# Three seams of layer 0: when the condition's SiLU, the latents' row sums and the next normalization's blocks are issued

## The chip, the cores and the metric

The kernel runs on one core of a Trainium2 chip, as one launch. The metric is device time in microseconds (us), the median of three runs. On the core, TensorE (PE in the profile; PEld is its loading of stationary operands) multiplies into PSUM, VectorE (DVE), ScalarE (ACT) and GpSimd (POOL) work on tiles in SBUF and PSUM, and SyncE (SP), POOL and ACT issue DMAs. Every engine takes its own instructions in a fixed order and waits on semaphores for the others.

## The reference

Two layers of a hybrid backbone over 1024 latent tokens and 256 context tokens, width 1024. Cut to layer 0, which the change touches, and to the start of layer 1:

```python
sh1, sc1, g1, sh2, sc2, g2 = split(silu(c) @ ada_w[0] + ada_b[0], 6)      # latents; context: the same with c_ctx
u = rms_norm(h, norm1_g[0]) * (1 + sc1) + sh1
y = concat(fourier_mix(u @ w_in), hyena_mix(u @ w_in)) @ w_out              # both streams
h = h + g1 * y
v = rms_norm(h, norm2_g[0]) * (1 + sc2) + sh2
h = h + g2 * ((silu(v @ w_gate) * (v @ w_up)) @ w_down)                      # FFN, inner width 2816 = 22 blocks of 128
u1 = rms_norm(h, norm1_g[1]) * (1 + sc1_of_layer_1) + sh1_of_layer_1         # layer 1: attention, FFN, final norm
```

`rms_norm` divides a token's row by the root of the mean of its squares.

## The kernel before

Activations lie transposed: 8 blocks (`b`) of 128 channels on the partitions, tokens along the free axis, in pieces `pc`: 0 and 1 are the two halves of the latents (512 tokens each), 2 is the context (256). Every operand of a product is split into a high part (`hi`, a cast to fp32r on ACT, line L350) and the rest (`lo = x - hi`, a subtraction on DVE, L352; `split`), and a product is three products: hi by hi, hi by lo, lo by hi. `weights` loads a block of weights into a staging tile and splits it; the parts are called `wh` and `wl` in the profile. `lin` (its products are L346) runs 8 blocks by 3 products, so 24 products a piece.

The program is one straight line, written with generators: a main loop calls `next()` on side work at chosen places. From the order in which instructions are traced, their dependencies and an estimate of their durations, a scheduler then fixes the order of each engine's instructions; `follow(x)` makes what is traced under it come behind instruction `x` on the engine of `x`.

Four stages of layer 0 matter here.

- **Output projection** (`out_proj`, 647 to 766 us in the profile). `inverse_last` ends the Hyena branch: its last operands `y` come from DVE sums (L1469 to L1475) and a split, so a cast on ACT, each. Then `out_proj` multiplies group 0, which is the context and latent half 0 together (products L1765, then L346), and group 1, latent half 1. `evict` (L1739) adds a result to `h` on DVE, and `square` (L609 on ACT, L614 on DVE) sums squares over the blocks. Each `fetch` takes one step of `late_groups`, which makes the modulation vector `m = 4` of layer 0: `load_cond` loads c and c_ctx into four broadcast tiles and applies SiLU to them on ACT (L556); then each of 8 blocks takes four row-wise products with sum on DVE (L584), with weights that POOL loads.
- **Second normalization.** `rms_begin` sums the squares over channels with 4 narrow products against a column of ones (`pq<-c,tk`), takes root and reciprocal; `rms_end` spreads the result to a 128-row tile (`pq<-t,c`, copied by ACT at L642). For latent half 1 both are called in `after1`, at the end of group 1, ahead of the FFN. `wino_first` and `wino_second` then form the FFN's operands of halves 0 and 1.
- **Context FFN** (22 blocks `fb`, 770 to 893 us): gate and up weights of each block, 24 products of 256 columns each, SiLU (L2011) and product (L2012). From `fb = 2` on, each block takes one step of `second`, the generator that runs `wino_second` (L1835, L1842, L1823 on DVE, a cast L1822 on ACT).
- **Context down projection** (1527 to 1595 us, products L2230): 22 blocks of 24 products, each with a weight block to split. `hook(kb)` takes one step of `after2(1)` in blocks 3, 6 and 8 on: the row sums, their spreading, and then the normalization of layer 1 for half 1, two of its 8 blocks in a step (`norm_block`: L656 on DVE, L658 on ACT, L659 on DVE).

Weight parts for the context FFN take tiles from the pools `wh`/`wl` (two each) and `ws` (four) in turn (`pair3`, counter `p3`).

Of the kernel before, what the change touches and what calls it, by code (L numbers as in the profile page):

```python
# [13 lines left out]
AF = mybir.ActivationFunctionType  # L14
# [244 lines left out]
class Builder:  # L259
# [333 lines left out]

    def late_groups(self, ms, where):

        self.load_cond(wide=where == "s4")
        for m in ms:
            yield from self.ada_group(0, m, (0, 1), where)

# [815 lines left out]
    def inverse_last(self, y, fl):  # L1415

        nc, a = self.nc, self.a
        V = nc.vector
        C, x, late = [], [], []

        def product(acc, first, cb, m, e, i, f):
            yh, yl = (q[:, cb * P:cb * P + P] for q in self.y_of(1, i, f))
            d = acc[cb][:, e * 256:e * 256 + 256]
            for k, (s, w) in enumerate(((yh, m[:, :256]), (yh, m[:, 256:]), (yl, m[:, :256]))):
                nc.tensor.matmul(d, s, w, start=cb not in first, stop=e == 1 and i == 1 and f == 3 and k == 2,  # L1425
                                 skip_group_check=True)
                first.add(cb)

        next(fl)
        for r in (0, 1):  # L1430
            acc = [self.PS() for _ in range(4)]
            first = set()
            ms = self.cmat2(a["vke_l"][r], True)
            for e, m in enumerate(ms):
                for cb in range(4):
                    for f in (0, 1):
                        product(acc, first, cb, m[:, f * 512:f * 512 + 512], e, 2 * e, 2 * r + f)
            yield
            if r == 0:
                next(fl)  # L1440
            else:
                for _ in fl:
                    yield
            ms = [self.cmat2(a["vko_l"][r, :, c:c + 2048], True) for c in (0, 2048)]
            if r:
                for cb in range(4):
                    x.append(self.S4())
                    self.ld(x[cb], self.xd[1][cb][:, :LAT])
            sa = [self.TK(), self.TK()]
            sa = [t[:, i:i + 256] for t in sa for i in (0, 256)]  # L1450
            for cb in range(4):
                for e, i in ((0, 3), (1, 1)):
                    for h, m in enumerate(ms[e]):
                        for f in (0, 1):
                            product(acc, first, cb, m[:, f * 512:f * 512 + 512], e, i, 2 * h + f)
                    if e == 0:
                        nc.scalar.copy(sa[cb], acc[cb][:, :256])
                A, B = sa[cb], acc[cb][:, 256:]
                t = self.G() if r == 0 else self.T()
                V.tensor_tensor(t[:, :256], A, B, ADD)  # L1460
                rv = t[:, 256:][:, ::-1]
                if r == 0:
                    V.tensor_tensor(rv, A, B, SUB)
                    C.append(t)
                    continue
                V.tensor_tensor(rv, B, A, SUB)
                y.t.update(self.new_act(pcs=(0, 1), wide=False, blocks=(4 + cb,)).t)
                v = self.T()
                V.tensor_tensor(v, C[cb], t, ADD)  # L1469
                V.tensor_tensor(C[cb], C[cb], t, SUB)  # L1470
                V.tensor_tensor(v, v, x[cb][:, :512], MUL)
                self.split(v, y.ap(0, 4 + cb, 0), y.ap(1, 4 + cb, 0))
            yield
        for cb in range(4):
            V.tensor_tensor(C[cb], C[cb], x[cb][:, 512:], MUL)  # L1475
            self.split(C[cb], y.ap(0, 4 + cb, 1), y.ap(1, 4 + cb, 1))

    def inverse_c(self, o, y):
        nc, a = self.nc, self.a
# [494 lines left out]
        s.to(2)  # L1974
        return s

    def ffn(self, l, u, h, hs, second, after, keep=None, begun={}):

        nc, a = self.nc, self.a
        n2 = NFB // 2  # L1980
# [19 lines left out]
        if l == 0:  # L2000
            self.pad(self.pt, PAD_T)
        if u is not None:
            for fb in range(NFB):
                wide = 3 if fb < NFB - 2 else 2
                gh, gl = self.weights(a["gate"][l, fb], wide=wide)
                uh, ul = self.weights(a["up"][l, fb], wide=wide)
                lo = self.last_lo
                ga = self.lin(gh, gl, 0, range(KB), u, (2,))[2]
                ua = self.lin(uh, ul, 0, range(KB), u, (2,))[2]
                t = self.T()  # L2010
                nc.scalar.activation(t[:, :256], ga[:, :256], AF.Silu)  # L2011
                nc.vector.tensor_tensor(t[:, :256], ua[:, :256], t[:, :256], MUL)  # L2012
                self.ldr(hidc[fb // 2][:, fb % 2], t[:, :256])
                if fb >= 2:
                    with self.follow(last):
                        next(second, None)
                last = lo
            self.load_cond(act=False)
            todo = (x for l1, m in [(0, 5)] + [(1, m) for m in range(6)]
                    for x in self.ada_group(l1, m, (0, 1) if l1 == 0 or m < 2 else (0,), "s4"))  # L2020
# [16 lines left out]
        for i in range(NFB // 2):  # L2037
# [26 lines left out]
            gate = dict(self.res)  # L2064
            for k in ((0, 0), (1, 1), (0, 1)):
                nc.scalar.activation(gate[k], gate[k], AF.Silu)
            t = self.G()
# [463 lines left out]
    def run(self):  # L2531
        nc, a = self.nc, self.a
# [9 lines left out]
        def drain(g):  # L2542
            for _ in g:
                pass

        u = Act()
# [90 lines left out]
        h = Act()  # L2637
        u = None

        def load_h(pcs):  # L2640
            for pc in pcs:
                for b, t in enumerate(self.load_x(pc)):
                    h.put(0, b, pc, t)

        uf = Act()
        hs0 = [self.DR([P, 1280]) for _ in range(KB)]
        hs1 = [self.DR([P, 1280]) for _ in range(KB)]

        def spill(h, hs, pcs):
            for pc in pcs:  # L2650
                for b in range(KB):
                    self.ldr(hs[b][:, pc * 512:pc * 512 + WID[pc]], h.ap(0, b, pc))

        rest = []

        def after1(pcs):
            spill(h, hs0, pcs)
            if 2 in pcs:
                uf.t.update(self.new_act(pcs=(2,)).t)
                rs = self.rms(pcs)  # L2660
                for b in range(KB):
                    self.norm_block({b: h.ap(0, b, 2)}, b, 2, 0, 3, uf, rs[0])
                load_h((1,))
                rest.append(rs[1])
            else:
                drain(first)
                rest.append(self.rms((1,))[0])

        def first_row():
            yield from self.wino_first(h, 0, 3, rest.pop())  # L2670

        first = first_row()

        load_h((2, 0))
        self.out_proj("w_out", y, [(2, 0), (1,)], h, 0, 2, after1, first, late)
        for b in range(8):
            self.tap(f"h1_{b}", h.ap(0, b, 0))
        u1 = Act()
        hd = [self.DR([P, LAT]) for _ in range(KB)]

        def after2(pc):
            c = self.rms_begin(pc)
            yield
            r = self.rms_end(pc, c)
            yield
            for b in range(KB):
                if b % 2 == 0:
                    u1.t.update(self.new_act(pcs=(pc,), blocks=(b, b + 1)).t)
                self.norm_block({b: h3.ap(0, b, pc)}, b, pc, 1, 0, u1, r)
                if b % 2:  # L2690
                    yield

        h3 = Act()
        self.ffn(0, uf, h3, hs0, (x for r in rest for x in self.wino_second(h, 0, 3, r)), after2, hd)
        for b in range(8):
            self.tap(f"h2_{b}", h.ap(0, b, 0))
        for i, _ in enumerate(self.values(u1)):
# [62 lines left out]
        for i, _ in enumerate(first_part(1)):  # L2760
            if i == 7:
                c = self.rms_begin(0)
# [53 lines left out]
        begun = {(0, 0): self.wino_begin(1, 0, 0, self.G)}  # L2816
        c = self.rms_begin(1)
# [87 lines left out]
```

## Time and profile before

| | |
|---|---|
| time, median of 3 runs (lowest, highest) | 2862.4 us (2861.56, 2863.65) |
| the profiled execution: time, span | 2867.56 us, 2865.8 us |
| granted TensorE clock, mean | 0.984 |
| busy: PE, PEld, DVE, ACT, POOL | 97%, 81%, 71%, 46%, 19% |
| 640.00 to 686.60 us: PE busy, clock | 43.61 of 46.60 us, 0.96 |
| 768.00 to 780.00 us: PE busy, clock | 11.39 of 12.00 us, 0.72 |
| 780.00 to 897.00 us: PE busy, clock | 117.00 of 117.00 us, 1.00 |
| 1545.00 to 1556.00 us: PE busy, clock | 8.00 of 11.00 us, 0.90 |

Times in the profile count from the first instruction. The clock is the share of its full speed that TensorE was granted in a stretch; at 0.50 a product takes twice as long. Columns of a stretch are, in order: from and to, length, then busy time and instructions of PE, PEld, DVE, ACT and POOL, the clock, the DMA share and GB/s.

### The profile page before, as it was taken

The numbers are of one execution on the slowest core, as the hardware profiler recorded it, in microseconds if no ns is written. First come the engines' busy times: TensorE is split into PE (matmuls) and PEld (weight loads), VectorE is DVE, ScalarE is ACT, GpSimd is POOL, SyncE is SP. The second block draws the span as 40 slices with busy tenths as digits, with TensorE's granted clock in tenths as the row PEclk, the third lists the DMA queues.
The fourth block names the chain that finished last, engine by engine and source line by source line (L and its number), as shares of the span: only waits on it lengthen the run. The fifth ranks groups of instructions, "written<-read, shape, count | busy, mean of one in ns | idle before, by whom it ended". The sixth has DMA issues, their size and how long they took to land.

```text
span 2865.8 us, 43630 instructions
## 1 busy us (share of the span) xinstructions
PE 2779.7 (97%) x15610; PEld 2325.6 (81%) x15610; DVE 2045.2 (71%) x3531; ACT 1321.0 (46%) x2269; POOL 543.2 (19%) x880
## 2 busy tenths in 40 slices
PE   7999999999999999999999999999999999999998
PEld 4876678788899888888888888888887788888887
DVE  6766777768777888866777536878867987655556
ACT  5433335443554333333455326888755533333434
POOL 2210234241001211222110002332212122112000
PEclk9999899999999999999999999999999999999999
DMA  7356525655556656658884436777856366434763
GB/s 267 120 167 214 158 83 190 220 172 219 204 189 210 207 192 200 212 196 328 308 308 154 147 120 143 195 203 200 227 199 215 122 242 224 144 110 167 234 195 133
DMA packets 296887, 554.21 MB, mean 193 GB/s; under 512 B 81872, under 2 KB 128658, under 8 KB 296670
## 3 DMA queue, kind: packets, MB, share of 16 engines
q1 hardware_dynamic: 232318, 361.06, 40.0%
q0 software_dynamic: 61504, 185.65, 18.6%
q10 hardware_dynamic: 2848, 4.72, 0.4%
q8 instruction: 123, 2.02, 0.3%
q14 instruction: 94, 0.77, 0.1%
HBM read 405.01 MB, written 118.76 MB: 183 GB/s over the span
## 4 chain that ended last, share of the span: by engine, by line
PE 71%; issue 3%; DVE 3%; DMA 2%; ACT 1%; POOL 1%; DVEq 0%; SPq 0%; POOLq 0%; ACTq 0%
PE ps L1932 25%; PE ps L346 15%; PE ps L2109 11%; PE pq L346 9%; PE pq L1932 3%; PE pq L2109 3%; PE ps L2230 2%; PE ps L2463 1%; PE ps L1425 1%; DMA s<-d 1%; DMA s<-in_c_ctx 1%; DMA g<-in_bias 0%; DMA s<-in_x_t 0%; DVE wl L352 0%; DVE s L352 0%
## 5 line engine op out<-in xcount | busy, mean ns | idle before, releaser
L1932 PE MATMUL ps<-s,s 128*128 128x512 f32 x2012 | 498.6, 391 | 3.3 <-DVE s L1823 1.7
L1932 PEld LDWEIGHTS ps<-s,s 128*128 128x128 f32 x2012 | 379.4, 189 | 83.9 <-DVE s L1823 2.6
L346 PE MATMUL ps<-s,wh 128*128 128x256 f32 (+1 forms) x1776 | 403.3, 331 | 6.0 <-ACT wh L350 2.5
L346 PEld LDWEIGHTS ps<-s,wh 128*128 128x128 f32 x1776 | 296.3, 191 | 41.3 <-ACT wh L350 3.4
L346 PE MATMUL ps<-s,wl 128*128 128x256 f32 (+1 forms) x888 | 267.1, 329 | 0.1
L2109 PE MATMUL ps<-s,s 128*128 128x512 f32 (+1 forms) x1000 | 259.7, 383 | 3.2 <-DVE s L352 3.1
L350 ACT CAST s<-s 128x1024 fp32r<-128x1024 f32 (+2 forms) x192 | 173.0, 926 | 192.0 <-DMA s<-d 172.3
L346 PE MATMUL pq<-s,wh 128*128 128x512 f32 (+1 forms) x848 | 260.9, 389 | 0.3 <-ACT wh L350 0.3
L352 DVE TENSOR_TENSOR wl<-ws,wh 128x1024 fp32r<-128x1024 f32 (+1 forms) x141 | 168.2, 1194 | 118.4 <-ACT wh L350 113.9
L350 ACT CAST wh<-ws 128x1024 fp32r<-128x1024 f32 (+1 forms) x141 | 144.7, 1026 | 204.4 <-PE ps L346 85.4
L346 PE MATMUL ps<-s,s 128*128 128x65 f16 (+4 forms) x2748 | 230.3, 235 | 6.3 <-DVE st L2446 2.6
L352 DVE TENSOR_TENSOR s<-s,s 128x1024 fp32r<-128x1024 f32 (+2 forms) x170 | 191.0, 1154 | 58.3 <-ACT s L350 58.2
L352 DVE TENSOR_TENSOR s<-t,s 128x512 fp32r<-128x512 f32 (+2 forms) x238 | 151.5, 652 | 104.6 <-ACT s L350 81.7
L350 ACT CAST s<-t 128x512 fp32r<-128x512 f32 (+2 forms) x238 | 133.8, 582 | 188.4 <-PE ps L1932 68.0
L2109 PEld LDWEIGHTS ps<-s,s 128*128 128x128 f32 x1000 | 184.4, 188 | 41.2 <-DVE s L352 4.8
L1932 PE MATMUL ps<-s,wh 128*128 128x512 f32 x624 | 194.8, 390 | 0.0
L346 PEld LDWEIGHTS ps<-s,wl 128*128 128x128 f32 x888 | 165.6, 190 | 16.6 <-DVE wl L352 0.6
L337 POOL DMA_DIRECT2D d<-s x186 | 101.4, 546 | 376.5 <-DVE s L1739 92.9
L346 PEld LDWEIGHTS pq<-s,wh 128*128 128x128 f32 x848 | 150.5, 189 | 22.8 <-issue 1.2
L346 PE MATMUL pq<-s,wl 128*128 128x512 f32 (+1 forms) x424 | 161.8, 382 | 1.3 <-DVE wl L352 1.3
L2109 PE MATMUL ps<-s 128*128 128x512 f32 (+1 forms) x500 | 150.7, 385 | 0.0
L346 PEld LDWEIGHTS ps<-s,s 128*128 128x128 f32 (+1 forms) x828 | 129.3, 192 | 22.3 <-issue 4.4
(487 smaller groups left out, 5485.8 us busy)
## 6 DMA issues: line engine op xcount, KB each, us to landing
s<-d SPq DMA_DIRECT2D x282, 256.0 KB, 3.9
d<-s POOLq DMA_DIRECT2D x170, 256.0 KB, 3.7
s<-in_down SPq DMA_DIRECT2D x150, 256.0 KB, 4.1
s<-in_ada_w POOLq DMA_DIRECT2D x64, 512.0 KB, 5.0
ws<-in_up SPq DMA_DIRECT2D x44, 512.0 KB, 3.7
d<-g POOLq DMA_DIRECT2D x86, 256.0 KB, 3.1
ws<-in_gate SPq DMA_DIRECT2D x42, 512.0 KB, 4.3
d<-tk POOLq DMA_DIRECT2D x66, 256.0 KB, 4.0
```

Source lines behind the costliest of these rows:

```text
L337: self.last_ldr = self.nc.gpsimd.dma_start(out, in_).ins
L346: self.last_mm = self.nc.tensor.matmul(o, l, r, start=st, stop=sp).ins
L350: self.last_hi = nc.scalar.copy(hi, src).ins
L352: self.last_lo = eng.tensor_tensor(lo, src, hi.bitcast(F32), SUB).ins
L1425: nc.tensor.matmul(d, s, w, start=cb not in first, stop=e == 1 and i == 1 and f == 3 and k == 2, skip_group_check=True)
L1932: nc.tensor.matmul(ps, x[:, sl], y, start=first and j == 0 and x is wh and y is xh, stop=j == 3 and x is wl, skip_group_check=True)
L2109: m = nc.tensor.matmul(acc[j][:, c0:c1], x[:, sl], y[:, xs], start=first and k == 0, stop=last and k == 2, skip_group_check=True)
L2230: m = nc.tensor.matmul(o, x[:, nb * P:(nb + 1) * P], t[:, c:c + 256], start=kb == 0 and k == 0 and nb % 2 == 0, stop=kb == NFB - 1 and k = ...
L2463: nc.tensor.transpose(ps[:, j * P:(j + 1) * P], src[:, j * P:(j + 1) * P], self.ident)
```

## The change

Three places of layer 0, all by the order in which work is traced; no product is added or removed.

1. `load_cond` in `late_groups` no longer applies SiLU. The SiLU comes three `fetch` steps later, and behind `inv_hi`, the last cast of `inverse_last`.
2. `rms_begin` and `rms_end` of latent half 1 move from `after1` into a new generator `second`, whose first two steps they are; each comes behind the last product traced so far (`last_mm`). `ffn` now takes a step of `second` from `fb = 0` on. The gate weights of `fb = 0` are loaded and split in step 6 of `wino_first` (`early`), still in `out_proj`; `p3 = 1` ahead of them gives them a pair of `ws` tiles.
3. In `after2(1)` a step normalizes one block, not two, and each block comes behind the `lo` of the block before on DVE.

```diff
     def late_groups(self, ms, where):
-        self.load_cond(wide=where == "s4")
+        self.load_cond(wide=where == "s4", act=False)
+        yield
+        yield
+        yield
+        with self.follow(self.inv_hi):
+            for t in self.cond:
+                for x in t:
+                    self.nc.scalar.activation(x, x, AF.Silu)
         for m in ms:
             yield from self.ada_group(0, m, (0, 1), where)
...
             self.split(C[cb], y.ap(0, 4 + cb, 1), y.ap(1, 4 + cb, 1))
+        self.inv_hi = self.last_hi
...
-    def ffn(self, l, u, h, hs, second, after, keep=None, begun={}):
+    def ffn(self, l, u, h, hs, second, after, keep=None, begun={}, early=()):
...
         if u is not None:
+            last = None
             for fb in range(NFB):
                 wide = 3 if fb < NFB - 2 else 2
-                gh, gl = self.weights(a["gate"][l, fb], wide=wide)
+                gh, gl = early.pop() if fb == 0 else self.weights(a["gate"][l, fb], wide=wide)
                 uh, ul = self.weights(a["up"][l, fb], wide=wide)
...
-                if fb >= 2:
-                    with self.follow(last):
-                        next(second, None)
+                with self.follow(last):
+                    next(second, None)
                 last = lo
...
-        rest = []
+        rest, early = [], []
...
                 drain(first)
-                rest.append(self.rms((1,))[0])
...
         def first_row():
-            yield from self.wino_first(h, 0, 3, rest.pop())
+            for k, _ in enumerate(self.wino_first(h, 0, 3, rest.pop())):
+                if k == 6:
+                    self.p3 = 1
+                    early.append(self.weights(a["gate"][0, 0], wide=3))
+                yield
...
             r = self.rms_end(pc, c)
             yield
+            los = []
             for b in range(KB):
                 if b % 2 == 0:
                     u1.t.update(self.new_act(pcs=(pc,), blocks=(b, b + 1)).t)
-                self.norm_block({b: h3.ap(0, b, pc)}, b, pc, 1, 0, u1, r)
-                if b % 2:
+                with self.follow(los.pop() if los and pc == 1 else None):
+                    self.norm_block({b: h3.ap(0, b, pc)}, b, pc, 1, 0, u1, r)
+                los.append(self.last_lo)
+                if b % 2 or pc == 1:
                     yield
 
         h3 = Act()
-        self.ffn(0, uf, h3, hs0, (x for r in rest for x in self.wino_second(h, 0, 3, r)), after2, hd)
+
+        def second():
+            with self.follow(self.last_mm):
+                c = self.rms_begin(1)
+            yield
+            with self.follow(self.last_mm):
+                r = self.rms_end(1, c)
+            yield
+            yield from self.wino_second(h, 0, 3, r)
+
+        self.ffn(0, uf, h3, hs0, second(), after2, hd, early=early)
```

The program keeps 15450 rows of PE, 3507 of DVE and 870 of POOL; ACT has 2187 rows where it had 2185, two more loads of an activation table, both in the context FFN. Away from the three places the engines' orders differ by a few rows only, at the very end of the program among them: there the 4 narrow products of the first of the last two row sums now stand 16 PE rows earlier.

Line numbers move: L609, L642, L656, L658, L659, L1739, L1822 before are L616, L649, L663, L665, L666, L1747, L1830 now.

On ACT at the end of the inverse (`s<-t` and `s<-g` are casts of `y`, `wh<-ws` casts of weights, rows with L556 or L603 the condition's SiLU), before:

```order
L350 CAST s_1523_6140<-t_6144 128x512
L556 ACT_TABLE_LOAD
L556 ACTIVATE s_1572_6234<-s_1572_6234 128x512 x2
L556 ACTIVATE s_1573_6239<-s_1573_6239 128x512 x2
L350 CAST s_1529_6178<-t_6182 128x512
L350 CAST s_1513_6066<-g_5480 128x512
L350 CAST wh_6356<-ws_6355 128x1024
```

and now:

```order
L350 CAST s_1523_6140<-t_6144 128x512
L350 CAST s_1529_6178<-t_6182 128x512
L350 CAST s_1513_6066<-g_5480 128x512
L350 CAST wh_6326<-ws_6325 128x1024
L350 CAST s_1519_6104<-g_5508 128x512
L350 CAST s_1525_6142<-g_5536 128x512
L350 CAST s_1531_6180<-g_5564 128x512
L603 ACT_TABLE_LOAD
L603 ACTIVATE s_1572_6234<-s_1572_6234 128x512 x2
L603 ACTIVATE s_1573_6237<-s_1573_6237 128x512 x2
```

The four SiLUs moved behind six casts, `s_1529`, which ends the operands of group 0, among them.

On PE, where the output projection meets the context FFN (`wh_7146` is its last weight, `pq` of width 1 the row sums, `ps` of 256 columns the gate products), before:

```order
L346 MATMUL ps_7219<-s_1531_6180,wl_7147 128x512
L346 MATMUL pq_7261<-c_91,tk_6978 128x1 x4
L346 MATMUL ps_7431<-s_1674_6862,wh_7420 128x256
L346 MATMUL ps_7431<-s_1675_6863,wh_7420 128x256
L346 MATMUL ps_7431<-s_1674_6862,wl_7421 128x256
```

and now, at the row sums' new place, 48 rows later (`ps_7440` are the up products of `fb = 0`, `ps_7489` the gate products of `fb = 1`):

```order
L346 MATMUL ps_7440<-s_1681_6869,wh_7410 128x256
L346 MATMUL ps_7440<-s_1680_6868,wl_7411 128x256
L346 MATMUL pq_7469<-c_91,tk_6978 128x1 x4
L346 MATMUL ps_7489<-s_1674_6862,wh_7478 128x256
L346 MATMUL ps_7489<-s_1675_6863,wh_7478 128x256
```

The row sums moved behind the 48 gate and up products of `fb = 0`. On ACT a little later, at the weights of `fb = 3` (`wh_7625`, its gate), before:

```order
L642 COPY t_7269<-pq_7274 128x512
L350 CAST wh_7558<-s_2061_7557 128x1024
L1822 CAST s_2069_7621<-s_1711_6980 128x512
L2011 ACTIVATE t_7547<-ps_7497 128x256
L350 CAST wh_7625<-s_2070_7624 128x1024
L1822 CAST s_2079_7692<-s_1725_7060 128x512
```

and now:

```order
L649 COPY t_7543<-pq_7548 128x512
L2020 ACTIVATE t_7613<-ps_7563 128x256
L1830 CAST s_2069_7621<-s_1711_6980 128x512
L1830 CAST s_2079_7692<-s_1725_7060 128x512
L350 CAST wh_7625<-s_2070_7624 128x1024
L350 CAST wh_7631<-s_2073_7630 128x1024
```

The gate weights of `fb = 3` now stand behind two casts of `wino_second`, and these behind the copy of the row sums.

On DVE in the context down projection (`wl` is a weight's low part, L656 or L663 the first step of a normalized block, L659 or L666 its last), before:

```order
L656 SCALAR_TENSOR_TENSOR t_14583<-s_3020_12687,c_99,t_14505 128x512
L656 SCALAR_TENSOR_TENSOR t_14587<-s_3021_12689,c_99,t_14505 128x512
L656 SCALAR_TENSOR_TENSOR t_14630<-s_3022_12691,c_99,t_14505 128x512
L656 SCALAR_TENSOR_TENSOR t_14634<-s_3023_12693,c_99,t_14505 128x512
L656 SCALAR_TENSOR_TENSOR t_14674<-s_3078_12968,c_99,t_14505 128x512
L659 SCALAR_TENSOR_TENSOR s_3328_14581<-t_14583,c_99,s_3328_14581 128x512
L352 TENSOR_TENSOR wl_14553<-ws_14551,wh_14552 128x1024
```

and now:

```order
L663 SCALAR_TENSOR_TENSOR t_14583<-s_3020_12687,c_99,t_14505 128x512
L666 SCALAR_TENSOR_TENSOR s_3328_14581<-t_14583,c_99,s_3328_14581 128x512
L352 TENSOR_TENSOR wl_14553<-ws_14551,wh_14552 128x1024
L663 SCALAR_TENSOR_TENSOR t_14624<-s_3021_12689,c_99,t_14505 128x512
L352 TENSOR_TENSOR wl_14596<-ws_14594,wh_14595 128x1024
L663 SCALAR_TENSOR_TENSOR t_14664<-s_3022_12691,c_99,t_14505 128x512
L666 SCALAR_TENSOR_TENSOR s_3329_14582<-t_14624,c_99,s_3329_14582 128x512
```

The weights' low parts moved ahead: two steps of the normalization stand before the first of them, six before.

## The prediction

> **What bounds the kernel now.** The page's first section comes first.
>
> ```profile
> PE 2779.7 (97%) x15610; PEld 2325.6 (81%) x15610; DVE 2045.2 (71%) x3531; ACT 1321.0 (46%) x2269; POOL 543.2 (19%) x880
> ```
>
> PE is the bound and the change keeps its products, so it can win only PE's idle time and the slow clock behind it. Then PE's waits, asked for each seam: between 636 and 686.5 us, 686.5 and 777.6, and 1300 and 1600 us (us in total, times, longest).
>
> ```profile
> PE ps L1765 <- ACT s L350: 2.3, 1, 2.3
> PE ps L1765 <- DVE wl L352: 0.3, 1, 0.3
> PE ps L1765 <- DVE s L1739: 0.3, 1, 0.3
> ...
> PE pq L346 <- DVE tk L614: 2.3, 1, 2.3
> ...
> PE ps L2230 <- DVE wl L352: 3.0, 2, 2.1
> ```
>
> Each seam has its own wait: a cast of `y`, the last sum of squares, a weight's low part. Then the view by stretches, which I laid on the steps of the clock; two late stretches without a seam stand at the end.
>
> ```profile
> 666.36:669.77 3.41, 1.32 (x8) 0.91 (x6) 0.00 (x0) 2.26 (x4) 0.00 (x0) 1.00 0.98 401
> 669.77:673.19 3.42, 3.23 (x9) 2.65 (x10) 3.25 (x9) 3.17 (x6) 0.00 (x0) 0.50 0.09 32
> 765.35:768.76 3.41, 1.12 (x7) 0.62 (x5) 1.44 (x2) 1.56 (x3) 0.54 (x1) 1.00 0.43 172
> 768.76:772.17 3.41, 3.41 (x17) 3.41 (x18) 2.99 (x4) 2.72 (x7) 0.00 (x0) 0.50 0.45 119
> 772.17:775.59 3.42, 3.42 (x18) 3.42 (x18) 1.99 (x3) 1.57 (x5) 0.00 (x0) 0.50 0.71 236
> 1547.00:1550.41 3.41, 2.50 (x22) 2.31 (x22) 3.41 (x5) 2.28 (x4) 0.00 (x0) 1.00 0.38 127
> 1550.41:1553.83 3.42, 1.32 (x13) 1.12 (x11) 3.42 (x6) 2.49 (x3) 0.00 (x0) 1.00 0.33 126
> 1553.83:1557.24 3.41, 3.41 (x16) 3.41 (x17) 3.41 (x5) 0.72 (x1) 0.00 (x0) 0.50 0.65 201
> 2072.65:2076.07 3.42, 1.92 (x10) 1.43 (x10) 2.77 (x6) 2.83 (x8) 2.89 (x6) 1.00 1.05 284
> 2157.99:2161.40 3.41, 2.08 (x10) 1.50 (x9) 3.41 (x7) 2.93 (x5) 2.14 (x5) 1.00 1.02 373
> ```
>
> A stretch of 3.41 us with PE busy 1.92 us or less is followed by one or two at clock 0.50; with 2.08 or 2.50 it is not (2157.99; 1547.00). So about 1.4 us of idle time within one stretch costs half of the next, 1.7 us, besides. The Trainium skill (TensorE: Matmul & The Clock Gate, section on why this matters) asks only that there be no idle gap over about 3 us. By that rule the gaps here would cost no clock; the rows show 0.50 behind gaps of 2.1 to 2.3 us, so the rows decide, and the rule is left as a rival below.
>
> **First seam: the SiLU, now behind the casts.** ACT, then DVE and PE:
>
> ```profile
> 657.99 1.28 ACT L556 ACT_TABLE_LOAD   x1
> 664.80 0.63 ACT L556 ACTIVATE s<-s 128x512 f32<-128x512 f32 x1 [5.53 <-DMA s<-in_c]
> 668.13 1.27 ACT L556 ACTIVATE s<-s 128x512 f32<-128x512 f32 x2 [0.78 <-DMA s<-in_c_ctx]
> 669.31 0.60 ACT L350 CAST s<-t 128x512 fp32r<-128x512 f32 x1
> ...
> 661.38 0.68 DVE L1471 TENSOR_TENSOR t<-t,s 128x512 f32<-128x512 f32 x1
> 683.21 0.75 DVE L584 CUSTOM_DVE_ANT_0 t<-s,s,c 128x512 f32<-128x512 f32 x1
> ...
> 683.88 1.53 DVE L1739 SCALAR_TENSOR_TENSOR s<-ps,c,s 128x256 f32<-128x256 f32 x3
> 691.14 1.22 DVE L352 TENSOR_TENSOR wl<-ws,wh 128x1024 fp32r<-128x1024 f32 x1
> ...
> 669.96 1.01 PE L1765 MATMUL ps<-s,wh 128*128 128x512 f32 x2 [2.28 <-ACT s L350]
> ```
>
> The last operand's sum is done at 662.1, but its cast stands behind SiLUs that wait for DMAs until 668.1. The Trainium skill agrees that ACT cannot pass a waiting instruction ("ACT/DVE are strict FIFO", same page, part 1). In the new order the cast runs at 662.1, and PE needs it at 667.7: the 2.28, the clock's 1.7 and the 0.3 behind it go, 4.3 in all.
>
> What is late next: the casts end about 666.8, table and SiLUs (1.28 + 4 x 0.59, since two took from 668.13 to 669.31) about 670.4, against 669.4 before, and the 32 products with sum (0.67 each in a row, 683.21 to 683.88) start then, three fetches later in the program, with evictions and weight parts between them. Counting DVE's new order from 670.4 (24 of the 32, 8 evictions of 0.5 (1.53 for three), 4 sums and one weight part, no idle time), the low part of the weights of `nb = 5` ends at 691.5; PE, without its stall, has reached them at about 690. Ahead of that, PE's order puts 4 products of `nb = 6` before the rest of `nb = 5`, whose weight tile is free only when `nb = 4` ends: about 0.6 and 0.45 us of idle time. Price from 0, if DVE is 2 us sooner, to 4.5, if SiLU is 2 us later and the clock falls too; I take 1.05, by the count. Loads by SP and POOL keep their order. Net -3.3.
>
> **Second seam: the row sums, now behind `fb = 0`.**
>
> ```profile
> 768.61 1.76 PE L346 MATMUL pq<-c,tk 128*128 128x1 f32 x8 [2.29 <-DVE tk L614]
> 770.22 0.77 PE L346 MATMUL ps<-s,wh 128*128 128x256 f32 x2
> 776.58 1.02 PE L346 MATMUL pq<-t,c 128*128 128x512 f32 x2
> ...
> 767.20 0.63 ACT L609 ACTIVATE tk<-s 128x512 f32<-128x512 f32 x1 [2.96 <-DVE s L1739]
> 767.74 1.97 ACT L350 CAST wh<-s 128x1024 fp32r<-128x1024 f32 x2
> 778.20 0.58 ACT L642 COPY t<-pq 128x512 f32<-128x512 f32 x1
> 780.33 0.62 ACT L1822 CAST s<-s 128x512 fp32r<-128x512 f32 x1
> ...
> 768.79 2.36 DVE L352 TENSOR_TENSOR wl<-s,wh 128x1024 fp32r<-128x1024 f32 x2 [0.24 <-ACT wh L350]
> 778.81 0.75 DVE L1835 SCALAR_TENSOR_TENSOR s<-s,c,t 128x512 f32<-128x512 f32 x1 [0.95 <-ACT t L642]
> 779.60 0.69 DVE L1842 TENSOR_TENSOR s<-s,s 128x512 f32<-128x512 f32 x1
> ...
> 780.00:897.00 117.00, 117.00 (x1018) 116.39 (x1018) 89.14 (x113) 61.65 (x87) 13.02 (x24) 1.00 0.63 201
> ```
>
> Away go 2.29 us of idle time and the half of 6.83 us at 0.50, 3.4; since part of that stretch is the narrow products, I take 3.2, together 5.5. The early gate weights are split while ACT and DVE wait for the last evictions, before 766. Two new waits follow, on base-trace times; a full-clock product takes 0.115 (last row).
>
> Gate products 766.2 to 768.9. The up weights are cast where the first weights were, after the last square: low part 768.8 to 770.0. PE waits 0.9. Then up to 772.5, row sums 773.4, `fb = 1` to 778.9, 11 products of `fb = 2`, and `rms_end` at 780.2. From there PE has 4.7 us of work to the gate of `fb = 3` at 784.9. The chain beside it: spreading 1.0, copy 0.6, two L1835 (0.67 each in a row), two L1842 with the casts behind them 1.7, and only then, in ACT's order, that gate's weights, 1.0: ready at 786.05, low part (behind two others on DVE) 787.25. PE waits 1.2, does two products, waits 1.0. Such 2.2 us in 2.4 us fall into one clock stretch to at least 1.4 us in about 7 of 10 positions of the stretches: 1.7 x 0.7 = 1.2. The Trainium skill calls this window free-running (same page, part 1); no row here shows where it will lie in another run. The two table loads more (1.28 each) lie in ACT time that waits for PE and cost nothing else. New 0.9 + 2.2 + 1.2 = 4.3, net -1.2; ends -4.6 (casts in time, only 0.9 left) and +1.0 (two stretches at half clock, 3.4 for the 1.2).
>
> **Third seam: one block a step.**
>
> ```profile
> 1548.69 0.38 PE L2230 MATMUL ps<-s,wl 128*128 128x256 f32 x1 [0.91 <-DVE wl L352]
> 1553.80 0.58 PE L2230 MATMUL ps<-s,wl 128*128 128x256 f32 x1 [2.10 <-DVE wl L352]
> ...
> 1543.44 3.40 DVE L656 SCALAR_TENSOR_TENSOR t<-s,c,t 128x512 f32<-128x512 f32 x5
> ```
>
> The five L656 in a row push the next low part behind PE. A block of the weights is 24 products, 2.7 us; DVE's share a block is now 1.14 + 2 x 0.67 = 2.5, in the order that PE asks. Followed row by row from 1543.4, one low part comes 0.25 us late. Away: 0.91 + 2.10 + 1.7 = 4.7, net -4.4; ends -4.7 and -2. Half 1 is normalized by about 1565, ahead of its first use after 1595.
>
> **Tail.** The narrow products 16 rows earlier can end this wait, which a late eviction may hold all the same: 0 to -0.6, I take -0.2.
>
> ```profile
> 2854.78 0.70 PE L346 MATMUL pq<-t,c 128*128 128x256 f32 x2 [0.58 <-DVE s L2130]
> ```
>
> **Sum.** -3.3 - 1.2 - 4.4 - 0.2 = -9.1: the profiled execution goes from 2867.6 to 2858.5. It lies 5.2 us above the median of the runs, so the median goes from 2862.4 to 2853.3.
>
> **Rivals.**
> - The second seam's chain is hidden (-4.6) and the first seam has no new wait (-4.3): -13.5, 2848.9. For it, the casts' rows start whenever ACT is free; against it, the order of the casts is fixed. Chance 0.17, with all between -11 and -13.5.
> - DVE holds the first seam back: SiLU 2 us later pushes that low part by as much, since DVE has no idle time before it. Then +0.2 there (4.5 new), and -5.6 in all, 2856.8; with the second seam at +1.0 it is -3.4, 2859.0. For it: c_ctx landed at 668.1, a nearly full DMA (0.98). Chance 0.20.
> - Slower: from `fb = 2` on, a step of `wino_second` stands in ACT's queue ahead of weights. DVE's share a step is 2 x 1.14 + 4 smaller ones, 4.5 us by the rows, against 5.5 of PE. If casts waiting on it made a step 6.3, 20 steps would lose 0.8 each, 16 us, and the change +7: 2869. It decides from 6.0 on. Against it: no PE idle in 117 us with the same work. Chance 0.04.
> - Gaps cost no clock, as the skill's rule has it: -2.58 + 1.05, -2.29 + 3.1, -3.0 + 0.25, -0.2 make -3.7, 2858.7. The 0.50 rows speak against it: 0.03.
>
> The forecast (-7 to -11) keeps 0.56. A measurement tells 0.2%, 5.7 us, from no change. Faster: 0.56 + 0.17 + some 0.02 of the second rival, 0.75; same 0.21; slower 0.04. From 2848.5 to 2859.0 the range holds all but the outer part of the rivals.
>
> **What would show it.** Right: no wait on L350 near 668 and no 0.50 there; PE idle near 690 (about 1), near 769 (0.9) and 785 us (2.2, on ACT `wh`, then DVE `wl`), all some 4 us earlier in the new trace; idle under 0.5 in the context down projection. Wrong: waits on `wh` at each step of the context FFN, a stall on L584's neighbours above 2 us, or a 0.50 where none stood.

## The result, and the profile after

The changed kernel takes 2857.5 us (median of 22 runs, 2849.7 to 2861.3) and the kernel before 2862.5 (22 runs, 2855.4 to 2871.1): ratio 0.9983, interval 0.9976 to 0.9990, or -5.0 us where -9.1 was forecast. The change is real and lies just within the 0.2% that the prediction called no change. The profiled execution took 2858.9 us, its span 2857.1. Its first section, and TensorE's waits in the three seams (640 to 690, 750 to 900 and 1530 to 1600 us; us in total, times, longest):

```profile
PE 2772.2 (97%) x15610; PEld 2321.2 (81%) x15610; DVE 2045.3 (72%) x3531; ACT 1323.8 (46%) x2271; POOL 541.9 (19%) x880
...
PE ps L1773 <- DVE wl L352: 0.3, 1, 0.3
...
PE ps L346 <- DVE wl L352: 1.5, 2, 0.8
PE ps L346 <- ACT wh L350: 0.6, 1, 0.6
...
PE ps L2238 <- DVE wl L352: 1.5, 2, 0.8
PE ps L2238 <- ACT wh L350: 1.1, 2, 0.7
```

All four waits of the profile before are gone (2.28 on the cast, 2.29 on the row sums, 0.91 and 2.10 on low parts), and no stretch between 640 and 2000 us has the clock at 0.50. In their place the second seam has three waits, 2.0 us, and the third four, 2.6 us; the first has no new one. One thing stands in no list of waits. The same 20 us of the context FFN, in the profile before and in the one after (TensorE busy throughout, at full clock in both):

```profile
800.00:820.00 20.00, 20.00 (x179) 20.00 (x178) 17.53 (x23) 9.89 (x14) 2.17 (x4) 1.00 0.48 158
```

```profile
800.00:820.00 20.00, 20.00 (x172) 20.00 (x171) 16.00 (x21) 10.51 (x15) 1.62 (x3) 1.00 0.59 183
```

The number in brackets is the count of products, with those under way at the edges: 179 before, 172 after. Of one product to the next that makes 113.3 ns before and 117.8 after (44 products took 4.99 and 5.18 us), so the 1000 products of this stage take 4.4 us more without a wait.

To compare executions, TensorE's 15610 products were counted in order, and the time taken between the starts of the same two of them (us; the columns from the third on are runs told below):

| products | before, first profile | before again | part 1 alone | part 3 alone | changed | changed again | with empty step |
|---|---|---|---|---|---|---|---|
| 2936 to 3249, first seam | 59.1 | 58.1 | 54.5 | 57.7 | 54.6 | 54.5 | 54.6 |
| 3527 to 4638, second seam and context FFN | 138.4 | 137.0 | 137.1 | 137.1 | 140.0 | 136.1 | 134.0 |
| 7501 to 7979, third seam | 63.1 | 60.1 | 60.1 | 59.8 | 60.2 | 59.9 | 60.7 |
| 15311 to 15599, tail | 57.0 | 57.0 | 56.2 | 56.3 | 56.3 | 56.3 | 56.3 |

The first profile of before is the dearest of its kind in each seam. That, and the spacing, are what the experiments are about.

### The profile page after: what moved, and what is told of

It is laid out like the page before. It is cut to its first block, busy times and chain, and to the rows that moved or that the text cites. A ratio compares the mean times of both kernels' runs of the same rounds, so it can differ in the third digit from the quotient of the medians.

```text
span 2857.1 us, 43635 instructions
## 1 busy us (share of the span) xinstructions
PE 2772.2 (97%) x15610; PEld 2321.2 (81%) x15610; DVE 2045.3 (72%) x3531; ACT 1323.8 (46%) x2271; POOL 541.9 (19%) x880
```

## The experiments

**The change executed again, and each part alone.** No edit in the first; then the diff's hunks for `load_cond` and `inv_hi` alone, those for `second` and `early` alone, and that for `after2` alone.

> The changed kernel, executed once more. Two profiled executions so far differ by more than the seams: in the context FFN (759 to 890 us) two products of 256 columns start 117.8 ns apart where they started 113.3 ns apart before, which costs 4.4 us. Theory A (the spacing belongs to the program): this execution shows 117.8 ns over the whole context FFN again, and the median lies about 5 us below before. Theory B (the spacing is drawn anew in each execution): it can show 113.3 ns, and then the FFN takes 4.4 us less. Both: no half clock between 640 and 2000 us, waits of about 0.7, 0.6 and 0.8 us near 763, 780 and 781 us.

> The kernel before with the first part alone (SiLU of the condition behind the casts of y). By the prediction's step: -3.3 us (4.3 away, 1.05 new near 690 us). By the profile of the changed kernel, in which the products from 640 to 690 us took 4.6 us less and no new wait stood near 690: -4.3 to -4.6 us in a profile whose seam fell to half clock before, and about 1 us less of a gain on the median, since not each execution need fall there. The spacing of the products in the context FFN stays at 113.3 ns if the second part made it 117.8 (theory A).

> The kernel before with the second part alone (row sums of half 1 behind the gate and up products of block 0, gate weights ahead). By the prediction's step: -1.2 us. Theory A: 5.2 us less between 760 and 781 us of before, 2.0 us of new waits, and 117.8 ns from product to product in the context FFN, 4.4 us more: about +1 us in all. Theory B (spacing by chance): the profile may show 113.3 ns, and the median is 1 to 3 us below before.

> The kernel before with the third part alone (normalization of layer 1, half 1, one block a step). By the prediction's step: -4.4 us, with 0.25 us of idle time left. By the profile of the changed kernel: -2.9 us, with four waits of 0.4 to 0.8 us (near 1553, 1554, 1569 and 1570 us here) that the prediction did not have, and a spacing of 113.3 ns instead of 117.8 in the second half of the stage, 1.4 us of the gain.

| | ratio to before | interval | us |
|---|---|---|---|
| whole change again | 0.9981 | 0.9972 to 0.9990 | -5.4 |
| part 1 alone | 0.9987 | 0.9977 to 0.9998 | -3.7 |
| part 2 alone | 1.0003 | 0.9990 to 1.0015 | +0.9 |
| part 3 alone | 0.9995 | 0.9986 to 1.0004 | -1.4 |

Here and below, us is the ratio's distance from 1 times the time before. Only part 1 is clear of noise. The parts add up to -4.2, but that sum says little. Each part run holds the tail's 0.7 us of the table, so it is counted three times; and part 2 alone made the scheduler move rows of layer 1, far from the three places. TensorE waited 3.6 us there for ACT, against 0.7 in the second profile of the kernel before, and two stretches at half clock followed. Part 2 alone, then that profile at the same place:

```profile
2272.54:2275.96 3.42, 0.48 (x3) 0.05 (x1) 3.42 (x6) 0.00 (x0) 1.08 (x2) 1.00 0.87 299
2275.96:2279.37 3.41, 2.71 (x6) 2.15 (x7) 2.66 (x5) 0.65 (x2) 2.47 (x5) 0.50 1.02 366
2279.37:2282.78 3.41, 3.41 (x9) 2.64 (x8) 0.00 (x0) 1.12 (x3) 0.22 (x1) 0.50 0.99 397
```

```profile
2271.16:2274.57 3.41, 3.41 (x15) 2.40 (x14) 3.41 (x6) 0.32 (x1) 1.08 (x2) 1.00 0.88 296
2274.57:2277.98 3.41, 2.73 (x13) 2.27 (x13) 2.70 (x5) 1.81 (x3) 1.48 (x3) 1.00 1.03 393
```

Products 13000 to 13100 took 29.4 us in that execution, and 23.7 to 24.0 in those of the kernel before, of the changed one and of parts 1 and 3 alone. So the +0.9 does not measure the second seam.

The whole change executed again showed the fast spacing from 782 us on, by the same view:

```profile
800.00:820.00 20.00, 20.00 (x179) 20.00 (x178) 16.49 (x22) 11.09 (x16) 1.65 (x4) 1.00 0.56 185
```

So theory A of the spacing falls: the same program shows both. Part 2 alone began the stage at 117.8 ns too and changed to 113.3 at 788.7 us, behind the last of its waits there.

**The kernel before, profiled again.**

> The kernel before, profiled once more. If what the forecast took from the first profile was typical: half clock behind all three seams (3.4, 6.8 and 3.4 us), waits of 2.28, 2.29, 0.91 and 2.10 us. If it was one draw of several, as the executions with one part of the change suggest: half clock at the second seam for 3.4 us, at the first not at all, waits of about 1 us and 1.5 us in the first seam, and 113.3 ns through the context FFN.

It took 2859.6 us, 8.0 less than in the first profile. The first SiLU on ACT, and TensorE's idle rows in the three seams:

```profile
660.15 0.63 ACT L556 ACTIVATE s<-s 128x512 f32<-128x512 f32 x1 [3.87 <-DMA s<-in_c]
...
665.94 0.61 PE L1765 MATMUL ps<-s,wh 128*128 128x512 f32 x2 [1.15 <-ACT s L350]
680.78 0.50 PE L1765 MATMUL ps<-s,wh 128*128 128x256 f32 x2 [1.53 <-DVE s L1739]
764.58 1.05 PE L346 MATMUL pq<-c,tk 128*128 128x1 f32 x8 [2.29 <-DVE tk L614]
1544.15 0.39 PE L2230 MATMUL ps<-s,wl 128*128 128x256 f32 x1 [0.91 <-DVE wl L352]
1549.27 0.38 PE L2230 MATMUL ps<-s,wl 128*128 128x256 f32 x1 [2.11 <-DVE wl L352]
```

The stretches of the clock around them:

```profile
663.48:666.89 3.41, 2.26 (x12) 1.62 (x11) 0.97 (x2) 2.77 (x5) 0.00 (x0) 1.00 0.98 401
666.89:670.31 3.42, 3.42 (x16) 2.82 (x16) 3.42 (x9) 2.03 (x4) 0.00 (x0) 1.00 0.05 17
762.47:765.88 3.41, 1.30 (x10) 1.19 (x10) 2.41 (x3) 2.71 (x5) 0.54 (x1) 1.00 0.25 100
765.88:769.29 3.41, 3.34 (x16) 3.24 (x16) 2.45 (x4) 2.97 (x7) 0.00 (x0) 0.50 0.58 189
769.29:772.71 3.42, 3.42 (x26) 2.94 (x26) 2.52 (x3) 2.62 (x4) 0.00 (x0) 1.00 0.57 187
1547.53:1550.95 3.42, 1.68 (x14) 1.69 (x15) 3.42 (x5) 1.86 (x3) 0.00 (x0) 1.00 0.20 31
1550.95:1554.36 3.41, 3.41 (x32) 3.41 (x31) 3.27 (x4) 1.05 (x1) 0.00 (x0) 1.00 0.94 341
```

One draw of several, then. In the first seam the condition's first transfer kept ACT waiting for 3.87 us and not 5.53, TensorE's wait on the cast was half as long, no half clock followed, and in its place TensorE waited 1.53 us for an eviction (0.3 in the first profile). The second seam paid for one stretch at 0.50 and not two. The third had its waits and no half clock behind them, and from there on 113.3 ns from product to product, where the first profile had 117.8 from 1557 to 1594 us. By the table these three seams took 1.0, 1.4 and 3.0 us less than in the first profile: 5.4 of the 8.0 us. Another 3.0 lay ahead of the first seam, where all versions do the same work: product 2936 starts 639.0 us into the first profile and 636.0 into the second, and between 635.4 and 640.9 us over all executions.

**Parts 1 and 3, without 2.**

> The kernel before with the first and the third part, without the second. So far: -3.7 us for the first alone, -1.4 for the third alone, +0.9 for the second alone, -5.0 for all. Theory A (the second part costs: 2.0 us of new waits, and a context FFN that begins at 117.8 ns from product to product in all three executions that held it): -5 to -6 us, as fast as the whole change or 1 us faster, with 113.3 ns through the context FFN. Theory B (the second part gains the 1.2 us of the prediction's step): -4, 1 us slower than the whole change.

0.9985 (0.9976 to 0.9995), -4.3 us, and 113.3 ns through the context FFN. The interval holds both theories. The whole change less this run leaves -0.7 to -1.1 us for part 2, within the noise; what it is worth stays open.

**Where the new waits of the third seam come from.** With the change SyncE issues the block loads of the context down projection in this order (`s` is block 9's staging tile, `ws` those of blocks 7, 8, 10, 11, 12):

```
ws_14551  ws_14594  ws_14672  ws_14710  ws_14753  s_14632
```

The edit puts block 10's load behind block 9's, and block 15's behind block 14's:

```diff
-                with self.follow(mark[0]), self.follow(mark[1]), self.follow(mark[2]):
+                with self.follow(self.last_ld if kb in (10, 15) else mark[0]), self.follow(mark[1]), self.follow(mark[2]):
```

> The changed kernel, with the loads of the down weights of blocks 9 and 14 of the context down projection issued ahead of those of blocks 10 and 15 and not behind two or three later blocks. Theory A (the four new waits of the third seam, 2.6 us, come from those two loads: they stand in SP's order behind loads that wait for a staging tile): the four waits go, the stage from 1545 to 1600 us of before takes 2.6 us less than in the changed kernel, -7 to -8 us against before. Theory B (the normalization's blocks on ACT and DVE hold the weights back, whatever the loads do): waits of 0.4 to 0.8 us on the casts and low parts stay, time as the changed kernel.

The changed kernel's rows around block 9, of DVE, SyncE's queue, ACT and PE:

```profile
1540.56 1.23 DVE L352 TENSOR_TENSOR wl<-ws,wh 128x1024 fp32r<-128x1024 f32 x1 [0.19 <-ACT wh L350]
...
1535.37 6.81 SPq L331 DMA_DIRECT2D ws<-in_down  x3
1542.28 0.42 SPq L331 DMA_DIRECT2D s<-in_down  x1
...
1546.95 1.05 ACT L350 CAST wh<-s 128x1024 fp32r<-128x1024 f32 x1 [1.04 <-DMA s<-in_down]
...
1548.05 0.50 PE L2238 MATMUL ps<-s,wh 128*128 128x256 f32 x2 [0.40 <-ACT wh L350]
1549.31 0.39 PE L2238 MATMUL ps<-s,wl 128*128 128x256 f32 x1 [0.76 <-DVE wl L352]
```

Block 12's load, the last of the three, waits until a `ws` tile is free, which block 7's low part on DVE decides at 1541.8; block 9's load, whose own tile is free long before (with the edit it goes out at 1530.15 us), stands behind it, lands 4.6 us later, and cast, low part and products follow from there. With the edit one wait is left in the stage:

```profile
1548.78 0.38 PE L2238 MATMUL ps<-s,wl 128*128 128x256 f32 x1 [0.29 <-DVE wl L352]
```

Theory A holds for the waits, 2.6 us to 0.3. The stage became only 1.8 us shorter (58.5 against 60.2), since its products from 1549 us on fell to 117.8 ns. In time there was nothing to see, 0.9994 (0.9983 to 1.0005): the edit made the scheduler move rows late in layer 1 too, where two waits grew by 1.6 us, first the changed kernel, then this one,

```profile
PE pq L1940 <- ACT g L1945: 1.7, 2, 1.0
```

```profile
PE pq L1940 <- ACT g L1945: 3.3, 2, 2.1
```

and half clock followed the longer one. Products 13000 to 13100 took 26.7 us for 23.7, and the tail fell back to 57.1 us, as in the kernel before. So the time says nothing about the loads; the waits do.

**The second seam mended.** The changed kernel, after 758 us, first ACT, then PE:

```profile
777.44 1.23 ACT L1830 CAST s<-s 128x512 fp32r<-128x512 f32 x2 [0.75 <-DVE s L1850]
778.57 3.89 ACT L350 CAST wh<-s 128x1024 fp32r<-128x1024 f32 x4
...
763.24 0.39 PE L346 MATMUL ps<-s,wl 128*128 128x256 f32 x1 [0.70 <-DVE wl L352]
779.66 0.50 PE L346 MATMUL ps<-s,wh 128*128 128x256 f32 x2 [0.57 <-ACT wh L350]
780.92 0.39 PE L346 MATMUL ps<-s,wl 128*128 128x256 f32 x1 [0.76 <-DVE wl L352]
```

Two edits: an empty step, and the up weights of block 0 split ahead (`early` then holds both):

```diff
                 r = self.rms_end(1, c)
             yield
+            yield
             yield from self.wino_second(h, 0, 3, r)
...
                     early.append(self.weights(a["gate"][0, 0], wide=3))
+                if k == 7:
+                    self.p3 = 3
+                    early.append(self.weights(a["up"][0, 0], wide=3))
```

> The changed kernel with two edits in its second seam: one empty step between rms_end and wino_second, so that two casts of the normalization no longer stand ahead of the weights of block 3, and the up weights of block 0 split ahead too, into a second pair of tiles. If the order on ACT is the cause (as the prediction had it): the waits of 0.70 us near 763, 0.57 near 779 and 0.76 near 781 go, 2.0 us. If instead the loads are late, waits on the casts stay. In time: -1 to -3 us against the changed kernel; the spacing of products in the context FFN stays a matter of chance, unless a pause is what sets it: then it may stay at 117.8 ns to the end, which takes 4.4 us back.

0.9969 (0.9958 to 0.9979), -8.9 us. The waits of 0.57 and 0.76 are gone; the 0.70 stayed, since the scheduler left the up weights' cast where it was. Then the empty step alone, and with it the load order of block 15 alone (`kb == 15` in the edit above), which moves nothing in layer 1:

> The changed kernel with the empty step between rms_end and wino_second alone, the other edit of the mended seam left out (with it the order on ACT came out the same but for one row, and its wait of 0.7 us stayed). Theory A (the empty step is the whole gain of 3 to 4 us: it removes the waits of 0.57 and 0.76 us and with them one chance that the products' spacing goes wrong): again 0.3% faster than before, waits near 779 and 781 gone. Theory B (half of that gain was the draw of the spacing and of the clock): -6 to -7 us against before.

> The same with the empty step, and the load of the down weights of block 14 ahead of that of block 15 on SP, which leaves the rest of the program's order but for one row. The waits of 0.67 and 0.76 us near 1564 should go and those near 1548 stay: -1.4 us against the run beside it, if the spacing falls alike; a measurement of this kernel can hardly tell that, the profile can.

The empty step alone: 0.9967 (0.9956 to 0.9978), -9.4 us. Its ACT rows have a cast of weights ahead of the normalization's two, at 776.62, and its only wait between 750 and 900 us is the old one:

```profile
776.62 1.03 ACT L350 CAST wh<-s 128x1024 fp32r<-128x1024 f32 x1
778.73 0.59 ACT L649 COPY t<-pq 128x512 f32<-128x512 f32 x1 [1.07 <-PE pq L346]
779.42 0.39 ACT L2020 ACTIVATE t<-ps 128x256 f32<-128x256 f32 x1
781.40 1.22 ACT L1830 CAST s<-s 128x512 fp32r<-128x512 f32 x2 [1.59 <-DVE s L1850]
...
PE ps L346 <- DVE wl L352: 0.7, 1, 0.7
```

All three executions with the empty step took 134.0 us from product 3527 to 4638, with 113.3 ns from 779 us at the latest; the changed kernel took 136.1 with the fast and 140.0 with the slow spacing. So the gain of 4 us over the changed kernel fits theory A, though the interval, -12.6 to -6.3 us, just reaches theory B's -6 to -7; and by these executions 2 us of it is there whatever the spacing. With the load the ratio is 0.9961 (0.9947 to 0.9975), -11.2 us, the lowest here and faster than both kernels. The waits of the third seam's second pair are gone, those of the first pair left:

```profile
1542.35 0.50 PE L2238 MATMUL ps<-s,wh 128*128 128x256 f32 x2 [0.21 <-ACT wh L350]
1543.61 0.39 PE L2238 MATMUL ps<-s,wl 128*128 128x256 f32 x1 [0.76 <-DVE wl L352]
```

Its third seam took 59.4 us against 60.7 in the run beside it, 1.3 less where 1.4 was expected; in time the two cannot be told apart.

**What sets the spacing.** Four narrow products behind four blocks, on the kernel before and on the changed one (there behind blocks 6, 10, 14 and 18). The next block's gate products come behind `pause`:

```diff
+                if fb in (4, 8, 12, 16):
+                    x = self.ident if fb < 10 else t[:, :P]
+                    pz = self.PQ()
+                    with self.follow(self.last_mm):
+                        for j in range(4):
+                            self.mm(pz[:, 2 * j:2 * j + 1], x, self.ones[:, 0:1], True, True)
+                    pause = self.last_mm
...
```

> The kernel before, with four narrow 128x1 products put behind blocks 4, 8, 12 and 16 of the context FFN: at 4 and 8 with operands that are ready, at 12 and 16 with one that SiLU and its product must first make, so that TensorE stands still for about 1 us; the next block's products come behind them. Their results go nowhere. Theory P (the spacing of 256-column products is drawn anew where the stream is broken): at one or more of the four places it changes between 113.3 and 117.8 ns and then stays until the next. Theory Q (it follows from the order or the tiles of the program): 113.3 ns throughout, as in the three executions of this order so far.

> The changed kernel with the four narrow products behind blocks 6, 10, 14 and 18 of the context FFN, at 14 and 18 with an operand that is late by about 0.5 us; their results go nowhere. With the same breaks the kernel before kept 113.3 ns. If a break can end the slow spacing, 117.8 ns, where an execution has it, it changes to 113.3 at one of them and stays there; if nothing but the start of the stage sets it, it goes on at 117.8 to the end, or is 113.3 from before block 6 on, which would tell nothing.

On the kernel before, between the breaks (the two first and the two last stretches):

```profile
776.00:796.00 20.00, 20.00 (x178) 20.00 (x178) 18.50 (x26) 11.39 (x16) 2.18 (x4) 1.00 0.47 155
800.00:820.00 20.00, 20.00 (x179) 20.00 (x178) 16.34 (x21) 10.51 (x15) 1.63 (x3) 1.00 0.48 158
822.00:842.00 20.00, 20.00 (x179) 20.00 (x178) 14.22 (x18) 10.54 (x15) 1.63 (x3) 1.00 0.64 209
846.00:866.00 20.00, 20.00 (x179) 20.00 (x179) 13.54 (x17) 11.35 (x16) 1.64 (x3) 1.00 0.63 205
```

On the changed kernel, ahead of block 6's break, and behind those of blocks 6, 10 and 14:

```profile
784.00:804.00 20.00, 20.00 (x173) 20.00 (x171) 19.48 (x27) 11.35 (x17) 1.62 (x3) 1.00 0.58 182
806.00:826.00 20.00, 20.00 (x178) 20.00 (x178) 14.83 (x20) 10.51 (x15) 1.62 (x3) 1.00 0.55 183
828.00:848.00 20.00, 20.00 (x179) 20.00 (x178) 14.25 (x18) 10.35 (x15) 1.62 (x3) 1.00 0.64 211
852.00:872.00 20.00, 20.00 (x172) 20.00 (x171) 11.51 (x15) 10.65 (x15) 1.62 (x3) 1.00 0.59 189
```

The first shows no change at any break (theory Q, so far); the second changes from slow to fast at block 6's break, which had no idle time, and from fast to slow at block 14's, which had 0.6 us. (The late operands cost 0.5 to 0.6 us at each of their breaks, where about 1 us was expected in the first of the two runs.) So a break in the stream can change the spacing, in either direction, and need not: theory P, with the order of the program no more than a tendency. Over all runs the kernel before's order of the second seam showed the fast spacing in 6 of 6 executions, the changed one began at the slow in 5 of 5 and still had it at 800 us in 3, and the one with the empty step had left it by 779 us in 3 of 3. In the context FFN of all these executions the spacing changed only at a wait, behind half clock or at narrow products. What in the hardware holds the state is open. The Trainium skill (TensorE: Matmul & The Clock Gate, section "Back-to-back issue gap") says that load and product together set the spacing of a stream; its table of gaps has one value for 256 columns, where the rows here show two.

## Why the prediction was right or wrong

The range held the time and the direction was right, but the most likely case, -7 to -11, was not what came. Step by step:

- **First seam, -3.3: -3.7 measured alone, the tail's 0.7 included, and -3.5 by the table against the second profile of before.** The size was right by two errors that cancel. The 1.7 us for the clock belonged to one execution; elsewhere a 1.53 us wait for an eviction stands in its place, which the change removes too. The new wait near 690 us (1.05) did not come, though it was close: in the new trace the low part ends at 689.06 us and TensorE takes up low parts again at 689.46. On the old time (1.9 us more) that is 691.0 where 691.5 was counted, and 691.4 where TensorE was put at 690. The count's 21.1 us came true, but not its pieces: they add up to more than 21.1 without the four sums, and in the trace 20 of the products, 6 evictions and 2 weight parts stand there. So the rival that had DVE hold this seam back is out, by 0.4 us.
- **Second seam, -1.2: no run measures it by itself.** Part 2 alone, +0.9 (-2.9 to +4.3), holds some 5.6 us lost in layer 1 in its profiled execution; the whole change less parts 1 and 3 leaves -0.7 to -1.1. Place and order of the three new waits were as forecast; the sizes were 0.70 for 0.9 and 1.33 for 2.2 (the terms listed for the gate of `fb = 3` end at 785.85 and not 786.05, which takes 0.2 off the 2.2), and the clock's 1.2 did not come in any of five executions. Against that, 5.5 "away" was 1.4 too much, since half clock for two stretches was one draw, and the spacing of products, in no term of the sum, costs up to 4.4 us. By the table against the second profile of before: -0.9 with the fast spacing, +3.0 with the slow.
- **Third seam, -4.4: this is the step that failed.** Against the second profile of before the table gives +0.1 and -0.2; alone it measured -1.4 (-4.0 to +1.1), the tail's 0.7 included. Of the forecast's 4.7 away, 3.0 were waits that do go, and 1.7 a half clock that came in 2 of 5 executions of this order. And 0.25 left was 2.6: "Followed row by row from 1543.4" followed DVE, and not SyncE, on which the change puts a block's load behind three later ones.
- **Tail, -0.2: -0.7 to -0.8** in each column of the table that holds any part of the change; the run with both loads moved kept 57.1 us. First before, then after, the rows with its waits (the 0.58 of before is in the prediction):

```profile
2858.03 1.22 PE L346 MATMUL pq<-t,c 128*128 128x256 f32 x2 [1.76 <-ACT t L638]
```

```profile
2847.23 0.83 PE L346 MATMUL pq<-c,tk 128*128 128x1 f32 x6 [0.47 <-ACT tk L2820]
2849.34 1.22 PE L346 MATMUL pq<-t,c 128*128 128x256 f32 x2 [1.28 <-ACT t L645]
```

- **From the profiled execution to the median.** The prediction subtracted 9.1 from an execution that lay 5.2 us above the median and carried the whole sum over to the median. That the excess lies elsewhere was assumed; 5.4 of the 8.0 us between the two profiles lay in the seams that the change takes away. With the second profile as the base, the whole change is -3.5, -0.9 or +3.0, 0 and -0.7: -5.1 with the fast spacing and -1.2 with the slow, and -5.0 was measured. That -5.1 and -5.0 agree is in part luck: one of the two profiles of the changed kernel had the slow spacing, and the second profile of before itself lay 2.0 us below the median beside it (2861.5).
- **Rivals.** That gaps cost no clock is refuted again: the 2.29 us gap was followed by 0.50 in each of six executions. The Trainium skill's rule of 3 us (TensorE: Matmul & The Clock Gate, section on why this matters) does not hold for them. Of the rival with the larger gain one half came, no new wait in the first seam, and the other did not, since the second seam's chain showed its waits. No wait of the context FFN recurred at each step, so the slower rival had nothing behind it.

## What to carry to other kernels

Before a profile's wait or half clock goes into a sum, ask how far that execution lies above the median: an excess of the size of the forecast gain may be the very thing that is about to be removed, and a second profile of the same kernel settles it. When a step moves earlier on one engine, follow the loads on their queue as well as the arithmetic, since a load that stands behind one that waits for a tile becomes the next wait. Where a new wait comes from two pieces of work in the wrong order, one empty step between them can be worth nearly as much as the change itself: here about 4 of the 9 us. And a part run alone is read by product number over the whole program, not by its total: here a wait in layer 1, 1500 us behind the seam, hid what the part was worth.

## What the runs showed of the hardware that was not expected

- Back-to-back products of 256 columns have two spacings at full clock, 113.3 and 117.8 ns, with no wait between. A stream keeps its spacing for up to 1000 products; a break can change it, and the same program shows both.
- The rule for the clock was drawn too sharply. Over all profiles, of the stretches of 3.41 us between 580 and 2840 us that ran at full clock themselves, each with TensorE busy for 1.45 us or less was followed by 0.50, none with 1.94 or more, and between the two 6 of 17, so busy time alone does not decide (1.68 at 1547.53 us above was not followed by it).
